# Attention kernel on one core: the last two key/value blocks are made within the first attention steps, and the second pair's queries wait in DRAM

## The chip, the cores and the metric

The kernel runs on 1 core of a Trainium2 chip. The metric is the device time of one execution in microseconds; lower is better. Matrix products run on TensorE (PE in the profile), the other engines are VectorE (DVE), ScalarE (ACT) and GpSimd (POOL). SyncE (SP) does no arithmetic here: it issues every DMA, in one queue, in order.

## The reference

It is one inference step of a streaming encoder with two layers, for a prompt of 1024 rows and a sample of 32 rows, of width 1024. Layer 0 is a matrix-memory mixer with an MLP. Layer 1 attends in chunks of 64 rows to keys and values that all layers of its kind would share; they are made from the output x of layer 0. Cut to the part that the change touches:

```python
kv = (x * (1 + kv_scale) + kv_shift) @ p['w_kv']          # 1024 -> 256 keys, 256 values
k_sh = kv[..., :KV_W].reshape(Bsz, S, NKV_B, HD_B)        # 4 heads of 64
v_sh = kv[..., KV_W:].reshape(Bsz, S, NKV_B, HD_B)
q = (u @ p['w_q_b'][lb]).reshape(Bsz, S, NH_B, HD_B)      # 16 heads of 64
...
s = jnp.einsum('bqkgd,bskd->bkgqs', qb, kb).astype(jnp.float32) * (HD_B ** -0.5) + bias
s = jnp.where(valid, s, -jnp.inf)
p = jax.nn.softmax(s, axis=-1).astype(vb.dtype)
return jnp.einsum('bkgqs,bskd->bqkgd', p, vb)
...
y = o @ p['w_out_b'][lb]
```

A chunk of queries sees its own chunk of keys and the eight before it, 576 keys at most, with a learned bias by relative position. The sample sees 512 cached keys and its own 32. The last 512 rows of keys and values, and the sample's, are outputs as well.

## The kernel before

**Tiles and parts.** Tokens lie in three blocks of 384, 384 and 288 columns (`TBS`); for keys and values in nine tiles of 128, the ninth holding the sample's 32 rows. A float32 factor is kept as a high part (a rounded copy, made by ACT) and a low part (the rest, made by DVE); `split` (L89, L90) makes both. A product is three matmuls: high by high, high by low, low by high. The three parts of a projection have lines L118 to L120.

**The stages around the change**, in order of time:

- *Queries*, L1412 to L1441. Eight strips of 128 columns, two heads each (`fc`, two to a weight block `pr`), are computed for three token blocks, first for the weight blocks 0, 1, 2 and then for 3. An eviction writes a high part (ACT, L1439) and a low part (DVE, L1440) into `QOT[ti]`, a tile for each token block. Meanwhile the norm that ends layer 0 runs for the next block on ACT (L889 to L891) and DVE (L892 to L896), stores x (L1401) and makes the block's inputs `U` (ACT L326 and L330, DVE L331).
- *Keys and values*, L1449 to L1526. Four blocks of `w_kv` are loaded and split into buffers of the tag "wc". For a tile t, `kv_input` loads x (L1482), scales it on POOL and shifts it on DVE, and splits it into `uk`, two tiles ahead. 48 products follow: for keys (i = 0) and then values (i = 1), for each of eight row blocks k, the three parts in turn (L1509, L1510, L1511). `put_keys` splits the keys (L1456, L1457), transposes them on PE (L1462) and copies them into `k0`, `k1` (L1467). `cached_keys` does the same with the cache, in every other tile. Tiles 4 to 8 store keys and values (L1523, L1524).
- *Bias*, L1541 and L1545: four tiles of the relative bias, in "wc" too.
- *Attention*, L1552 to L1664. The four key heads form two pairs (`gp`), `e` counts within a pair. `softmax_unit` makes scores (L1558), adds the bias with the maximum (DVE, L1569), the exponential (ACT, L1572), the reciprocal (L1573) and the scaling (POOL). `transposed` turns the probabilities round on PE (L1588) and copies them out (ACT L1596 for e = 1, DVE L1598 for e = 0). `weighted_values` multiplies by the values (L1608) and writes over the queries (L1613, L1614).
- *Output projection*, from 1632 us on.

**Buffers.** The pool `ring` has 3 buffers "raw" and 6 buffers "wc". Of the eight banks of PSUM, attention uses two double ones for scores, three for transposes (tag "pt") and one for values.

**What sets the order.** Side work is written as generators that `flow.tick` moves on between steps. In attention PE's order is the written one (`manual_schedule`): a group of scores is added, and older groups move on by one step, to transposes and values; chunks alternate between wide ones (8, 12, 13, ...) and slim ones (7, 6, 5, ...), all for the first pair and then all for the second. Everything else is ordered by the scheduler of the language, by priorities and free buffers.

## Time and profile before

| what | us |
|---|---|
| median of 3 runs (lowest, highest) | 2479.54 (2476.41, 2479.93) |
| profiled execution, its own time | 2479.81 |
| its span | 2478.0 |
| queries, within the span | 1263.5 to 1359.3 |
| keys and values | 1359.3 to 1422.0 |
| attention | 1422 to 1632 |

The times are of whole executions. The span runs from the first to the last recorded instruction of one profiled execution, whose granted clock of TensorE was 0.992 of full speed on average. Places in the text ("at 1423") are microseconds from the start of this span. The page of the profile gives totals, groups of instructions by line, and the chain of work that ended last; an answer of the trace gives the same for a stretch of time.

### The profile page before, as it was taken

The numbers are of one execution on the slowest core, as the hardware profiler recorded it, in microseconds if no ns is written. First come the engines' busy times: TensorE is split into PE (matmuls) and PEld (weight loads), VectorE is DVE, ScalarE is ACT, GpSimd is POOL, SyncE is SP. The second block draws the span as 40 slices with busy tenths as digits, with TensorE's granted clock in tenths as the row PEclk, the third lists the DMA queues.
The fourth block names the chain that finished last, engine by engine and source line by source line (L and its number), as shares of the span: only waits on it lengthen the run. The fifth ranks groups of instructions, "written<-read, shape, count | busy, mean of one in ns | idle before, by whom it ended". The sixth has DMA issues, their size and how long they took to land.

```text
span 2478.0 us, 42688 instructions
## 1 busy us (share of the span) xinstructions
PE 2413.7 (97%) x16844; PEld 2315.4 (93%) x16844; DVE 1759.7 (71%) x4038; ACT 1016.9 (41%) x2118; POOL 168.6 (7%) x315
## 2 busy tenths in 40 slices
PE   7999999999999999999999999999999999999997
PEld 4999999999999999999999867789999999899997
DVE  4899999788679679677597667746853442776758
ACT  4644456382211212212266556654754443221212
POOL 0211100000000000000001134410000000000003
PEclk9999999999999999999999989999999999999999
DMA  8433224313224224234122310050375646767632
GB/s 297 122 110 101 84 88 129 107 35 119 77 87 137 84 86 135 80 92 142 43 98 82 91 40 1 18 147 27 134 251 212 215 179 254 262 239 273 255 130 72
DMA packets 236220, 318.10 MB, mean 128 GB/s; under 512 B 11624, under 2 KB 185084, under 8 KB 234996
## 3 DMA queue, kind: packets, MB, share of 16 engines
q1 hardware_dynamic: 236020, 315.38, 38.8%
q8 instruction: 132, 2.16, 0.4%
q14 instruction: 68, 0.56, 0.1%
HBM read 242.79 MB, written 74.91 MB: 128 GB/s over the span
## 4 chain that ended last, share of the span: by engine, by line
PE 78%; DVE 8%; DMA 6%; ACT 2%; issue 1%; POOL 0%; SPq 0%; DVEq 0%; POOLq 0%; ACTq 0%
PE up L118 10%; PE up L120 10%; PE up L119 9%; PE dn L1283 9%; PE dn L119 5%; PE dn L118 5%; PE dn L120 5%; DMA fx<-hd 3%; PE pv L1608 2%; PE pt L1588 2%; PE s L1558 2%; PE o L118 1%; PE o L119 1%; PE o L120 1%; PE op_b L118 1%
## 5 line engine op out<-in xcount | busy, mean ns | idle before, releaser
L120 PE MATMUL up<-u,w_up 128*128 128x264 f32 x1024 | 292.9, 286 | 0.0
L118 PE MATMUL up<-u,w_up 128*128 128x264 f32 x1024 | 292.4, 286 | 0.0
L119 PE MATMUL up<-u,w_up 128*128 128x264 f32 x1024 | 291.1, 284 | 0.0
L1283 PE MATMUL dn<-fx,wf 128*128 128x264 f32 x2208 | 275.3, 286 | 7.9 <-DMA fx<-hd 7.4
L1283 PEld LDWEIGHTS dn<-fx,wf 128*128 128x128 f32 x2208 | 272.2, 189 | 9.7 <-issue 4.6
L119 PE MATMUL dn<-h,w_dn 128*128 128x384 f32 (+1 forms) x768 | 249.5, 325 | 0.0
L118 PE MATMUL up<-U,w_up 128*128 128x384 f32 (+1 forms) x768 | 249.2, 324 | 0.0
L119 PE MATMUL up<-U,w_up 128*128 128x384 f32 (+1 forms) x768 | 247.9, 323 | 0.0
L118 PE MATMUL dn<-h,w_dn 128*128 128x384 f32 (+1 forms) x768 | 247.8, 323 | 0.0
L120 PE MATMUL up<-U,w_up 128*128 128x384 f32 (+1 forms) x768 | 247.6, 322 | 0.0
L120 PE MATMUL dn<-h,w_dn 128*128 128x384 f32 (+1 forms) x768 | 247.3, 322 | 0.0
L119 PEld LDWEIGHTS up<-u,w_up 128*128 128x128 f32 x1024 | 193.9, 189 | 0.0
L118 PEld LDWEIGHTS up<-u,w_up 128*128 128x128 f32 x1024 | 193.8, 189 | 0.0
L120 PEld LDWEIGHTS up<-u,w_up 128*128 128x128 f32 x1024 | 193.3, 189 | 0.0
L986 DVE SCALAR_TENSOR_TENSOR ACC<-dn,ada,ACC 128x264 f32<-128x264 f32 (+4 forms) x328 | 131.7, 426 | 86.4 <-PE dn L1283 74.6
L238 DVE SCALAR_TENSOR_TENSOR aacc<-rada,cs,aacc 128x256 f32<-128x256 f32 x448 | 190.3, 477 | 0.0
L986 DVE SCALAR_TENSOR_TENSOR acc<-dn,ada,acc 128x384 f32<-128x384 f32 (+2 forms) x256 | 119.4, 486 | 47.4 <-PE dn L120 46.3
L1025 ACT ACTIVATE r<-up 128x384 f32<-128x384 f32 (+1 forms) x96 | 44.3, 463 | 246.9 <-PE up L120 238.4
L119 PEld LDWEIGHTS dn<-h,w_dn 128*128 128x128 f32 x768 | 144.4, 188 | 0.2 <-DVE h L1028 0.2
L120 PEld LDWEIGHTS dn<-h,w_dn 128*128 128x128 f32 x768 | 144.5, 188 | 0.0
L120 PEld LDWEIGHTS up<-U,w_up 128*128 128x128 f32 x768 | 144.3, 188 | 0.0
L118 PEld LDWEIGHTS up<-U,w_up 128*128 128x128 f32 x768 | 144.2, 188 | 0.1
(354 smaller groups left out, 5957.4 us busy)
## 6 DMA issues: line engine op xcount, KB each, us to landing
hd<-HL SPq DMA_DIRECT2D x28, 1848.0 KB
raw_up<-in_w_up_dram SPq DMA_DIRECT2D x68, 512.0 KB
rada<-in_w_ada_dram SPq DMA_DIRECT2D x64, 512.0 KB
fx<-hd SPq DMA_DIRECT2D x37, 528.0 KB
raw_dn<-in_w_down_dram SPq DMA_DIRECT2D x36, 512.0 KB
ada_room<-in_w_ada_dram SPq DMA_DIRECT2D x32, 512.0 KB
fx<-hd SPq DMA_DIRECT2D x50, 264.0 KB
fx<-hd SPq DMA_DIRECT2D x16, 792.0 KB
```

The costliest lines, as they stand in the source:

```text
L118: nc.tensor.matmul(ps, wh, mov(0, k), start=(k == 0), stop=False)
L119: nc.tensor.matmul(ps, wh, mov(1, k), start=False, stop=False)
L120: nc.tensor.matmul(ps, wl, mov(0, k), start=False, stop=(k == nk - 1))
L238: nc.vector.scalar_tensor_tensor(acc[:, cnd], raw[:, k], sc, acc[:, cnd], op0=ALU.mult, op1=ALU.add)
L986: nc.vector.scalar_tensor_tensor(xs, ps[:, off + o:off + o + mm_], gate[:, fc, cnd:cnd + 1], xs, op0=ALU.mult, op1=ALU.add)
L1025: nc.scalar.activation(r, ps[:, :n], AF.Relu)
L1283: nc.tensor.matmul(p, ws[w][:, wl, k], t[:, s0, xl], start=first and k + n_ == 0, stop=k == kg - 1 and n_ == 2, skip_group_check=not first)
L1558: nc.tensor.matmul(s[:, b, :w], qst, kk[i][:, g, k0 + j0:k0 + j0 + w], start=(i == 0), stop=(i == 1))
L1588: nc.tensor.transpose(pt[:kp, j - j0, pr * P:(pr + 1) * P], ps_[pr][:, j * P:j * P + kp], ident)
L1608: nc.tensor.matmul(pv[64 * e:64 * e + 64, :nq], V[:kp, vt0 + j, g * 64:(g + 1) * 64], pts[e][:kp, j, :nq], start=(j == 0), stop=(j == nt - 1))
```

## The change

It does five things.

1. The weight blocks of the queries come in the order 2, 3, 0 and then 1. `QOT[ti]` is laid out so that each pair's queries lie together. The second pair's queries (high and low) are stored to DRAM (`qd`, 1.57, 1.57 and 1.31 MB) as soon as its last strip is evicted.
2. The blocks of `w_kv` are loaded and split into the room that those queries left, not into "wc" buffers. So more inputs `uk` fit.
3. The stage of keys and values makes only tiles 0 to 6 (`LATE = 7`). In a tile, the 32 products with high parts of x go first, then the 16 with low parts. Cached keys come one per tile.
4. Tiles 7 and 8 are made in pieces of 6 products within the first attention steps. `fill` is called at each group of a step and puts out a piece at every second call. Their accumulator, `KVB`, takes one bank of the three that transposes had.
5. Only two bias tiles are loaded at first. When the pieces are done, `second_pair` gives the bank back as a third room ("pt3"), loads the second pair's queries back and loads the other two bias tiles. The first block of output weights is loaded one step earlier and split one step later.

```diff
+    qd = [dr.tile([P, 2, 6 if ti < 2 else 5, 256], F32, name=f"qd{ti}") for ti in range(3)]
+    def qo(c, gp):
+        return QOT[c // 6][:, gp, :, c % 6, :]
...
+    def kv_block(pr, half, dst):
+        nm = f"kv{pr}_{half}"
+        raw = raw_tile([P, 4, 256], f"raw_{nm}")
+        nc.sync.dma_start(raw, a["w_kv"][512 * half:512 * half + 512, 256 * pr:256 * pr + 256].rearrange(
+            "(k p) c -> p k c", p=P))
+        split(dst[0], dst[1], raw)
+        wkv[pr, half] = dst
+    def rooms(ti, n):
+        flat = QOT[ti][:, 1].rearrange("p e c x -> p (e c x)")
+        return [flat[:, i * 1024:(i + 1) * 1024].rearrange("p (k c) -> p k c", k=4) for i in range(n)]
+    for gi, grp in enumerate(((2, 3, 0), (1,))):
...
+                if fc == 7:
+                    nc.sync.dma_start(qd[ti], QOT[ti][:, 1].bitcast(F32))
                 flow.tick(n / 96)
+            if gi:
+                if ti == 0:
+                    r0 = rooms(0, 3)
+                    kv_block(0, 0, r0[0:2])
+                elif ti == 1:
+                    r1 = rooms(1, 3)
+                    kv_block(0, 1, r1[0:2])
+                    kv_block(1, 0, (r0[2], r1[2]))
+                else:
+                    kv_block(1, 1, rooms(2, 2))
...
-    wkv = [[wblock(f"kv{pr}_{half}", a["w_kv"], 512 * half, 256 * pr) for half in range(2)] for pr in range(2)]
...
-    uks = [kv_input(0), kv_input(1)]
+    uks = {t: kv_input(t) for t in range(2)}
+    LATE = 7
...
+    def kv_mm(pk, uk, i, k, part):
+        w = wkv[i, k // 4]
+        if part == 0:
+            nc.tensor.matmul(pk, uk[:, 0, k], w[0][:, k % 4], start=(k == 0), stop=False)
+            nc.tensor.matmul(pk, uk[:, 0, k], w[1][:, k % 4], start=False, stop=False)
+        else:
+            nc.tensor.matmul(pk, uk[:, 1, k], w[0][:, k % 4], start=False, stop=(k == KC - 1))
...
+    def late_keys(kd, t, m, pos):
+        yield
+        put_keys(kd, bank(f"kt_n{t}"), m, pos)
+    for t in range(LATE):
+        if t < 4:
+            flow.add(cached_keys(t))
+        m, pos, vi, dk, dv, r0 = kv_place(t)
...
+        for part in range(2):
+            for i in range(2):
+                for k in range(KC):
+                    kv_mm(pk[i], uk, i, k, part)
+                if i != part:
+                    flow.tick()
+        kd = [tmp_t([P, 256], f"kd{i}_n{t}", F32R) for i in range(2)]
+        split_keys(kd, pk[0], m)
+        flow.add(late_keys(kd, t, m, pos))
...
+    psX_cm = tc.tile_pool(name="psX", bufs=1, space=PSUM, reuse_waits="tile")
+    KVB = psX_cm.__enter__().tile([P, 2, 256], F32, name="KVB")
+    def kv_tile(t):
+        m, pos, vi, dk, dv, r0 = kv_place(t)
+        uk = uks.pop(t)
+        for i in range(2):
+            pk = KVB[:, i]
+            for k in range(KC):
+                kv_mm(pk, uk, i, k, 0)
+                kv_mm(pk, uk, i, k, 1)
+                if k % 2 == 0:
+                    continue
+                if k == KC - 1 and i == 0:
+                    work = raw_tile([P, 4, 256], f"kd_{t}")
+                    kd = kd_of(work)
+                    split_keys(kd, pk[:m], m)
+                    nc.scalar.copy(work[:m, 2], pk[:m])
+                    put_rows(dk, r0, m, work[:m, 2])
+                elif k == KC - 1:
+                    nc.scalar.copy(V[:m, vi], pk[:m])
+                    put_rows(dv, r0, m, V[:m, vi])
+                yield
+                if k == 3 and i == 1:
+                    put_keys(kd, psT.tile([P, 2, 256], F32, tag="pt", name=f"kt_n{t}", bufs=2).rearrange(
+                        "p i c -> p (i c)"), m, pos)
+                    yield
+        done_kv.add(t)
+    def kv_pieces():
+        for t in range(LATE, NT):
+            yield from kv_tile(t)
+    done_kv = set(range(LATE))
+    pieces = kv_pieces()
+    fills = [0, 0.0]
+    def fill(share):
+        if fills[0] is None:
+            return
+        fills[1] += share
+        while fills[0] < fills[1]:
+            if next(pieces, fill) is fill:
+                fills[0] = None
+                return
+            fills[0] += 1
...
-    for i, (nb, ns) in enumerate(((3, 0), (3, 0), (2, 1), (0, 3))):
+    def bias_tile(i):
+        nb, ns = ((3, 0), (1, 2))[i % 2]
...
+    bias_tile(0)
+    bias_tile(1)
+    nun = [0, 0]
+    psY = []
...
+            nun[1] += 1
+            if psY and nun[1] % 3 == 0:
+                pt = psY[0].tile([P, 2, 256], F32, tag="pt3", name=f"pt_{nm}_{e}_{j0}", bufs=1)
+            else:
+                pt = psT.tile([P, 2, 256], F32, tag="pt", name=f"pt_{nm}_{e}_{j0}", bufs=2)
             js = range(j0, min(nt, j0 + 2))
+            if j0 == 4:
+                fill(0.5)
...
+        if nt <= 4:
+            fill(0.5)
...
+        fill(0.5)
         pts[gp, c, e] = transposed(pr_, wid, e, nm)
         yield
         if e:
+            fill(0.5)
...
+    def second_pair():
+        psX_cm.__exit__(None, None, None)
+        psY_cm.append(tc.tile_pool(name="psY", bufs=1, space=PSUM, reuse_waits="tile"))
+        psY.append(psY_cm[0].__enter__())
+        for ti in range(3):
+            nc.sync.dma_start(QOT[ti][:, 1].bitcast(F32), qd[ti])
+        bias_tile(2)
+        bias_tile(3)
...
+                while not gp and min(c // 2, 8) not in done_kv:
+                    fill(1.0)
                 for e in range(2):
                     flow.add(att_group(gp, c, e))
                     flow.tick()
-                if gp and i in (8, 11):
-                    wo_pre[0, len(wo_pre)] = wo_block(0, len(wo_pre))
+                    if fills[0] is None and not psY:
+                        second_pair()
+                if gp and i in (7, 10):
+                    wo_raw = raw_tile([P, 4, 256], f"raw_ob0_{len(wo_pre)}")
+                    for dst, src in wo_srcs(wo_raw, 0, len(wo_pre)):
+                        nc.sync.dma_start(dst, src)
+                if gp and i in (9, 12):
+                    w = ring.tile([P, 2, 4, 256], F32R, tag="wc", name=f"w_ob0_{len(wo_pre)}", bufs=6)
+                    split(w[:, 0], w[:, 1], wo_raw)
+                    wo_pre[0, len(wo_pre)] = w
```

The number of evictions, score products, softmaxes and transposes stays the same.

On ACT, in the queries' stage, around the norm of the third token block. In the names, `w1_n01_2` is that norm's work, `QO0` the queries of the first token block, and `raw_kv0_0` the first weight block of keys and values. Before:

```order
L330 ACTIVATE ut_n01_1_7_0_13407<-acc0_1_5247,comb_92 128x384
L889 ACTIVATE w1_n01_2_13415<-var_n01_2_13412,eps_ln_75 128x288
L1439 CAST QO0_13196<-q_5_0_13440 64x6x64
L890 ACTIVATE w1_n01_2_13415<-w1_n01_2_13415 128x288
L891 ACTIVATE w1_n01_2_13415<-w1_n01_2_13415 128x288
```

And after:

```order
L330 ACTIVATE ut_n01_1_7_0_13411<-acc0_1_5247,comb_92 128x384
L889 ACTIVATE w1_n01_2_13419<-var_n01_2_13416,eps_ln_75 128x288
L1458 CAST QO0_13199<-q_1_0_13444 64x6x64
L890 ACTIVATE w1_n01_2_13419<-w1_n01_2_13419 128x288
L89 CAST QO0_13199<-raw_kv0_0_13979 128x1024
L891 ACTIVATE w1_n01_2_13419<-w1_n01_2_13419 128x288
```

The cast of the weight block now stands between two instructions of the norm, and it writes into the tile from which the second pair's queries are stored.

On PE, at the start of attention. `s_0_7_01` are scores of pair 0, chunk 7, e = 0, second half of the heads; `pt_0_8_0_0` is a transposed tile of chunk 8; `k0`, `k1` are the keys, `uk_7` the input of tile 7. Before:

```order
L1558 MATMUL s_0_8_11_14966<-k1_14101,QO1_13490 128x288
L1558 MATMUL s_0_7_00_14977<-k0_14100,QO1_13490 128x512
L1558 MATMUL s_0_7_00_14977<-k1_14101,QO1_13490 128x512
L1558 MATMUL s_0_7_01_14986<-k0_14100,QO1_13490 128x512
L1558 MATMUL s_0_7_01_14986<-k1_14101,QO1_13490 128x512
L1588 MATMUL pt_0_8_0_0_14996<-ident_64,p_0_8_00_14938 128x128
```

And after:

```order
L1666 MATMUL s_0_7_00_14832<-k0_14123,QO1_13494 128x512
L1666 MATMUL s_0_7_00_14832<-k1_14124,QO1_13494 128x512
L1666 MATMUL s_0_7_01_14841<-k0_14123,QO1_13494 128x512
L1666 MATMUL s_0_7_01_14841<-k1_14124,QO1_13494 128x512
L1541 MATMUL KVB_14775<-QO0_13199,uk_7_14667 128x256
L1542 MATMUL KVB_14775<-QO0_13199,uk_7_14667 128x256
L1544 MATMUL KVB_14775<-QO0_13199,uk_7_14667 128x256
```

The first piece (6 products in all, these three lines twice) stands between the scores and the transposes; further pieces follow in the same way, the last of the 16 pieces within the steps of chunks 14 and 5.

On SP, the bias loads and the last stores of keys (`ks`) and values (`V`). Before:

```order
L1523 DMA out_dram<-ks_14804 128x256
L1541 DMA bias_14913<-bias_d 64x3x576
L1524 DMA out_dram<-V 128x256
L1541 DMA bias_14913<-bias_d 64x3x576
L1523 DMA out_dram<-ks_14889 32x256
L1541 DMA bias_14916<-bias_d 64x3x576
L1524 DMA out_dram<-V 32x256
```

And after:

```order
L1548 DMA ck_14436<-in_cache_k_dram 128x256
L1646 DMA bias_14776<-bias_d 64x3x576 x2
L1646 DMA bias_14779<-bias_d 64x576
L1536 DMA out_dram<-V 128x256
L1646 DMA bias_14779<-bias_d 64x576
L1650 DMA bias_14779<-bias_d 32x2x544
L1536 DMA out_dram<-ks_14569 128x256
```

The first bias tile now stands ahead of every store of keys and values, and the second among the first of them.

More of the change, by code (lines that the diff above doesn't have):

```diff
@@ L1467, in put_keys, with kd_of @@
                     KCOPY[i][half != g0](dst, ps[64 * g0:64 * g0 + 64, i, :, :m])
+    def kd_of(work):
+        return [work[:, i].bitcast(F32R) for i in range(2)]
     ck, cv = a["cache_k"][0].rearrange("s g d -> s (g d)"), a["cache_v"][0].rearrange("s g d -> s (g d)")
@@ L1546, in trunk_kernel @@
                               bias_d[h0:h0 + 4 * ns - 3:4, :32, :544].rearrange("h i j -> i h j"))
-        bias += [b3[:, j] for j in range(nb)]
-        sbias += [s3[:, j] for j in range(ns)]
-    nun = [0]
+        bias.extend(b3[:, j] for j in range(nb))
+        sbias.extend(s3[:, j] for j in range(ns))
+    bias_tile(0)
+    bias_tile(1)
+    nun = [0, 0]
+    psY = []
     def softmax_unit(qst, g, k0, nk, bt, off, nm):
```

83 lines of the change are left out of this document (38 added, 45 removed).

## Prediction

> **What bounds the kernel now.** I read the page's engine totals first, then the busy time of each engine in the stages that the change touches, then PE's waits there, then the chain of work and the timeline at the points where a term is needed.
>
> ```profile
> PE 2413.7 (97%) x16844; PEld 2315.4 (93%) x16844; DVE 1759.7 (71%) x4038; ACT 1016.9 (41%) x2118; POOL 168.6 (7%) x315
> ```
>
> PE is busy for 97% of the span, so what counts is work taken off PE's path and the few places where PE stands still. By stage (us, then PE, PEld, DVE, ACT and POOL busy with their counts, granted clock, DMA share, GB/s):
>
> ```profile
> 1263.50:1359.30 95.80, 95.07 (x585) 93.61 (x584) 78.10 (x143) 62.92 (x135) 7.24 (x3) 1.00 0.31 95
> 1359.30:1422.00 62.70, 58.60 (x486) 57.56 (x484) 42.96 (x79) 34.41 (x88) 12.09 (x6) 1.00 0.35 91
> 1422.00:1440.00 18.00, 11.51 (x49) 8.77 (x49) 10.21 (x35) 8.67 (x24) 5.71 (x8) 0.70 0.66 150
> 1440.00:1530.00 90.00, 87.54 (x654) 64.90 (x653) 62.54 (x224) 57.65 (x166) 36.64 (x72) 0.98 0.00 1
> 1530.00:1632.00 102.00, 97.59 (x722) 71.68 (x721) 74.35 (x262) 69.10 (x198) 43.39 (x84) 1.00 0.08 18
> ```
>
> These are the queries' projection, the keys and values, the start of attention, and attention's two halves. PE is full in the first. In the second it loses 4.1 us. In the third it loses 6.5 of 18 us, and its clock falls to 0.70. PE's waits in the second stage and, below, at the start of attention:
>
> ```profile
> PE kv L1511 <- DVE uk L90: 4.1, 4, 2.1
> PE s L1558 <- DVE mx L1569: 4.1, 2, 3.1
> PE pt L1588 <- DVE pT L1598: 1.7, 1, 1.7
> ```
>
> The chain of waits says what the longest of them, 3.1 us, hangs on: a bias tile, whose load starts after the last store of values.
>
> ```profile
> 1423.54 6.78 DMA bias<-bias_d
> 1430.48 0.76 DVE L1569 CUSTOM_DVE_ANT_0 p<-s,bias 128x576 f32<-128x576 f32 x1 [2.45 <-DMA bias<-bias_d]
> 1431.30 1.22 PE L1558 MATMUL s<-k,QO 128*128 128x512 f32 x2 [3.15 <-DVE mx L1569]
> ```
>
> **The change part by part.** All terms are made against the profiled execution's 2479.81 us (its span is 2478.0), 0.27 us above the median of 2479.54, so the sum is not corrected. I call "same" what lies within 0.2% (4.96 us): about what a measurement of this kernel can tell from no change.
>
> *Term 1: the keys' and values' stage gets shorter.* Tiles 7 and 8 leave it: 2 × 48 products and 2 × 4 transposes of keys, 104 PE instructions. Their spacing comes from a full stretch of this stage, the first of these rows (the others serve terms 3 and 4):
>
> ```profile
> 1400.00:1420.00 20.00, 20.00 (x171) 20.00 (x170) 13.74 (x28) 12.08 (x34) 0.00 (x0) 1.00 0.27 70
> 1422.10:1444.50 22.40, 15.99 (x73) 11.33 (x73) 11.95 (x40) 10.44 (x27) 7.20 (x10) 0.70 0.53 120
> 1444.50:1480.00 35.50, 35.17 (x259) 26.72 (x258) 26.20 (x86) 22.64 (x62) 14.29 (x28) 1.00 0.00 1
> ```
>
> 20.00 / 171 = 117 ns, and 104 × 117 ns = 12.2 us. The products with high parts now go first, so a product with a low part (L1511 waits for it, 4.1 us) has 32 others ahead of it, 32 × 117 ns = 3.7 us, more than the longest single wait of 2.1: I take the 4.1 as gone. Late next is DVE: it still makes all nine inputs here, so its 42.96 us now stand against some 46 us of PE rather than 62.7, and cached keys come every tile, not every other. PE lost 4.1 us at 69% DVE; at over 90% it can lose between nothing and as much again; I take 1.5, under half, since inputs 0 to 5 no longer wait for the weights' buffers. Term: −12.2 − 4.1 + 1.5 = −14.8 (−16.3 to −12.2).
>
> *Term 2: the queries' stage.* Three stores (1.57, 1.57 and 1.31 MB) join it. At a DMA share of 0.31 they have room. But the first weight block of keys and values is now split in the room that the first store must leave:
>
> ```profile
> 1294.18 0.56 DVE L1440 TENSOR_TENSOR QO<-q,QO 64x384 fp32r<-64x384 f32 x1
> 1296.13 0.55 SPq L1401 DMA_DIRECT2D xsp<-acc  x1
> 1297.00:1302.00 5.00, 5.00 (x29) 4.82 (x28) 3.66 (x8) 4.94 (x10) 0.00 (x0) 1.00 0.87 315
> 1301.35 0.45 ACT L890 ACTIVATE w_n<-w_n 128x288 f32<-128x288 f32 x1
> 1301.83 0.45 ACT L891 ACTIVATE w_n<-w_n 128x288 f32<-128x288 f32 x1
> 1319.09 0.19 DVE L331 TENSOR_TENSOR U<-ut_n,U 128x32 fp32r<-128x32 f32 x1 [0.19 <-ACT ut_n L330]
> 1319.73 0.29 PE L118 MATMUL q<-U,w_q 128*128 128x288 f32 x1
> 1328.33 1.05 ACT L89 CAST w_kv<-raw_kv 128x1024 fp32r<-128x1024 f32 x1 [0.38 <-PE q L120]
> 1329.47 1.23 DVE L90 TENSOR_TENSOR w_kv<-raw_kv,w_kv 128x1024 fp32r<-128x1024 f32 x1
> ```
>
> The split costs ACT 1.05 us and DVE 1.23 us and stood, before, in quiet water at 1328. It now stands on ACT between L890 and L891 of the third block's norm (1301.8). Behind L891 on the same engine stand evictions of q and the inputs U, and PE needs the last U at 1319.73, 0.45 us after it is made (1319.28). The store can be issued when the fourth strip is evicted (1294.74); with the 0.9 us that the store of 1296.13 took to its first packets and 1.57 MB at 315 GB/s (5.0 us) it lands near 1300.7, before the split. Then U comes later by between 1.05 and 2.3 us, say 1.7; less 0.45 of slack that is +1.3 (0 to +6). The upper end is the next store sharing the 315 GB/s: 3.15 MB take 10.0 us, landing near 1305.7 to 1307, some 5 later.
>
> *Term 3: start of attention.* Only two bias tiles are loaded here, ahead of the last stores, so the 3.15 us wait goes. The stretch from the first score product to the end of the first chunk's values:
>
> ```profile
> 1422.14 0.80 PE L1558 MATMUL s<-k,QO 128*128 128x288 f32 x4
> 1438.02 1.45 PE L1588 MATMUL pt<-ident,p 128*128 128x128 f32 x10 [1.73 <-DVE pT L1598]
> 1441.20 3.35 PE L1608 MATMUL pv<-pT,V 128*64 128x256 f32 x20
> ```
>
> takes 1422.14 to 1444.55, 22.4 us. It has 15.99 us of PE work at a clock of 0.70; at full clock that would be 11.2, so 4.8 us hang on the clock. Fewer stops should win back half of it, 2.4. Into it come three pieces of 6 products, 18 × 117 ns = 2.1 us, half of them in what is left of the waits (1.73 here, the first softmaxes), leaving 1.05. Term: −3.15 − 2.4 + 1.05 = −4.5. Bounds: the whole clock and pieces all hidden, −8.0; clock as bad as before, with the pieces in full and at half speed, 0.
>
> The Trainium skill, "TensorE: Matmul & The Clock Gate", section "HAM oscillation — how this bites in real kernels", gives the shorthand "no PE-idle gaps >~3.4µs" for keeping full clock. The trace does not agree: the clock is at 0.70 here though the longest gap is 3.15 us. By that rule the start of attention, with no gap near it after the change, would run at full clock, and term 3 would be −8.0; this is within rival B.
>
> *Term 4: the moved work comes back.* Of the 96 products and 8 transposes 86 run after the first values: 86 × 117 ns = 10.1 us on PE. What they can hide in is the share of the chain that isn't PE:
>
> ```profile
> by line: PE pv L1608 36.4%; PE s L1558 24.9%; PE pt L1588 22.1%; DVE pT L1598 7.9%; issue 4.0%; DVE p L1569 3.2%; ACT QO L1613 0.8%; DVE QO L1614 0.6%; DVE mx L1569 0.4%; DVE mx L1573 0.2%
> ```
>
> PE holds 83.4% between 1440 and 1485; 16.6% of the 35.5 us of the row above is 5.9 us. A piece stands at a fixed place in PE's order, not at the stall, so I let 60% of this be filled: 3.5. Term: +6.6 (+4.2 to +10.1).
>
> *Term 5: two rooms for transposes.* The accumulator of the pieces takes the third room until they are done. Which steps that meets: chunks 8, 12 and 13 with six tiles each, 7, 6 and 5 with four, 30 tiles. A room is free again when its copy ends:
>
> ```profile
> L1598 DVE COPY pT<-pt 128x512 f32<-128x512 f32 x20 | 13.6, 684 | 2.4 <-PE pt L1588 2.4
> L1596 ACT COPY pT<-pt 128x512 f32<-128x512 f32 x20 | 11.5, 584 | 22.5 <-PE pt L1588 22.4
> ```
>
> With two rooms PE may run one copy ahead; a piece stands before each third tile (or behind the second), 6 × 117 = 702 ns, and covers the copy of the first. So most tiles pay nothing, and I take 2.0: 30 × 67 ns, a tenth of a copy (0 to +19, the worse end being a whole copy per tile: 15 × 684 + 15 × 584 ns). A few products of pieces also wait for the accumulator's eviction; that is inside it.
>
> Costed at nothing: the reload of the second pair's queries, 4.46 MB or 14.2 us at 315 GB/s, issued when the pieces end near 1480 and first needed at about 1530 by the second pair; the row 1440 to 1530 shows the DMA engines at 0.00. Without that cover it would cost up to 14 us. The two last bias tiles ride behind it (6.78 us above). The load of the output weights moves one step, in attention's second half at a DMA share of 0.08; its splits move one step the other way, among DVE's 74.35 of 102 us. If SP's queue sticks at the pieces' stores, only these loads wait behind it.
>
> Sum: −14.8 + 1.3 − 4.5 + 6.6 + 2.0 = −9.4, so 2479.8 − 9.4 = 2470.4 us.
>
> **The rivals.**
> B, a larger gain: the clock stays up and the pieces fill the stalls. −14.8 + 1.3 − 8.0 + 4.2 + 0.5 = −16.8: 2463.0. For it: the 3.15 us gap was the longest, and pieces stand where PE waited for copies. Against: the half clock lasted here through much shorter gaps too.
> C, the gain is eaten: the pieces lie wholly on the path and the clock is as bad as before. −14.8 + 1.3 + 0 + 10.1 + 2.0 = −1.4: 2478.4. For it: PE shows 35.17 of 35.50 us busy from 1444.5 on.
> E, the queries' store lands late and stops ACT in the norm: term 2 is 5.6 rather than 1.3, the rest as forecast: 2474.7. Against: the store of tile 0 is issued ahead of the next.
> D, slower: the third room was what kept PE going. Each of the 30 tiles waits a whole copy, 19.0 instead of 2.0: 2487.4. It decides (over 2484.8) from (4.96 + 11.4) / 30 = 0.55 us a tile on. For it: DVE's copies already hold 7.9% of the chain with three rooms, and pieces add evictions to DVE and ACT. Against: ACT stands idle 22.5 us before its 20 copies, and the pieces themselves give them time.
>
> **How the numbers follow.** Forecast (A) 0.40, own range 2466 to 2475; B 0.20; C 0.14; E 0.08; D 0.18. Faster by over 0.2% (below 2474.9) are B, 0.36 of A and half of E: 0.60. Within 0.2%: C, the rest of A and of E, and a little of D: 0.23. Slower: 0.17, nearly all of D. The range takes B in to 2460 and D to 2486; beyond lie perhaps 0.05 below and 0.12 above.
>
> **What the profile of the changed kernel would show.** Term 1: the stretch of keys and values near 48 us with no wait for a low part; with several us of waits for inputs, DVE is the new bound there. Term 2: a wait of PE for U at the third block, 1 to 2 us; over 4 is E. Term 3: no wait for a bias, and a clock above 0.8 in the first 18 us of attention. Term 4: the time from the first values to the last piece, against 83% PE in the chain before. Term 5: waits of transposes for L1710 and L1712, a sum of some 2 us; from 16 on D holds. I am wrong if the first half of attention grows by more than the 15 us which the stage before gives up.

## The result and the profile after

The changed kernel takes 2488.61 us (median of 6; 2484.68 to 2490.34) against 2479.66 us before (6 runs): the ratio is 1.0038, with a 95% interval of 1.0026 to 1.0051. It is slower by 9 us; 2470.4 was forecast, with a range of 2460 to 2486. The profiled execution took 2490.34 us, with a span of 2488.6.

Where the time went is read from PE's timeline: the first product of each stage marks its start. In the profiled executions of this document, of kernels written alike up to the queries, the queries begin between 1262 and 1266 us, so stages are compared by their lengths. "Start of attention" runs from the first score product to the first values product of the eighth chunk (chunk 4); it holds all pieces. In brackets is the stretch of term 3, from the first score product to the end of the first chunk's values. Forecast and measured are differences to before.

| stage, us | before | after | forecast | measured |
|---|---|---|---|---|
| queries | 95.7 | 96.0 | +1.3 | +0.3 |
| keys and values | 62.8 | 55.9 | -14.8 | -6.9 |
| start of attention (first chunk) | 64.2 (22.4) | 75.3 (16.5) | +4.1 (-4.5) | +11.1 (-5.9) |
| rest of attention | 145.6 | 148.9 | 0 | +3.3 |
| output projection | 100.2 | 100.4 | 0 | +0.2 |
| sum | 468.6 | 476.6 | -9.4 | +8.1 |

The busy times by stretch of the changed kernel, in the columns of the prediction's table:

```profile
1265.70:1361.70 96.00, 95.31 (x584) 93.49 (x583) 79.29 (x140) 62.84 (x130) 10.29 (x5) 1.00 0.46 152
1361.70:1417.60 55.90, 47.31 (x382) 46.70 (x380) 39.57 (x75) 30.57 (x81) 7.04 (x4) 0.94 0.35 91
1417.60:1435.00 17.40, 15.53 (x97) 12.21 (x98) 11.93 (x38) 10.26 (x25) 7.20 (x10) 0.90 0.02 7
1435.00:1478.00 43.00, 38.18 (x297) 31.39 (x295) 26.24 (x82) 24.11 (x65) 12.16 (x23) 1.00 0.21 80
```

Keys and values have 382 PE instructions instead of 486, as counted, but PE is busy for only 47.3 of 55.9 us: 8.6 us idle, twice the 4.1 of before. The start of attention is busier (15.5 of 17.4 us) at a clock of 0.90 rather than 0.70. While the pieces run, from 1435 to 1478, PE stands still for 4.8 of 43 us, where before it stood still for 0.3 of 35.5 us (the prediction's row from 1444.5 on). PE's waits in these two stages, first from 1361 to 1425, then from 1425 to 1480:

```profile
PE kt_n L1493 <- ACT kd_n L1485: 6.6, 1, 6.6
PE s L1666 <- DVE k L1498: 3.3, 2, 2.1
```

```profile
PE pt L1702 <- DVE pT L1712: 2.3, 4, 0.8
PE pt L1702 <- DVE k L1498: 1.6, 1, 1.6
PE KVB L1541 <- ACT kd L1606: 1.2, 2, 0.6
PE pt L1702 <- ACT pT L1710: 0.4, 2, 0.2
```

**The one wait of 6.6 us.** The wait for low parts (4.1 us) is gone, and a longer one has taken its place: the first key transposes wait for the high part of the keys. The timelines of DVE, ACT and PE, in this order, show on what that hangs:

```profile
1365.24 0.55 DVE L1459 TENSOR_TENSOR QO<-q,QO 64x384 fp32r<-64x384 f32 x1
1367.76 1.23 DVE L1522 TENSOR_TENSOR x<-x,kvss 128x1024 f32<-128x1024 f32 x1 [1.97 <-POOL x L1521]
1369.02 0.56 DVE L1459 TENSOR_TENSOR QO<-q,QO 64x384 fp32r<-64x384 f32 x1
1370.79 1.23 DVE L1522 TENSOR_TENSOR x<-x,kvss 128x1024 f32<-128x1024 f32 x1 [1.21 <-POOL x L1521]
1372.04 0.42 DVE L1459 TENSOR_TENSOR QO<-q,QO 64x256 fp32r<-64x256 f32 x1
...
1378.58 0.19 DVE L1459 TENSOR_TENSOR QO<-q,QO 64x32 fp32r<-64x32 f32 x1 [0.25 <-ACT QO L1458]
```

```profile
1372.49 0.18 ACT L1458 CAST QO<-q 64x32 fp32r<-64x32 f32 x1 [5.80 <-DVE QO L1459]
1378.57 0.37 ACT L1485 CAST kd_n<-kv 128x256 fp32r<-128x256 f32 x1
```

```profile
1379.00 1.15 PE L1493 MATMUL kt_n<-ident,kd_n 128*128 128x128 f32 x4 [6.57 <-ACT kd_n L1485]
```

The last query product ended at 1361.9, but its evictions on DVE end at 1378.8: they stand, in DVE's order, behind the shifts (L1522) of inputs 5 and 6, and these wait for POOL. ACT's evictions wait for DVE's, and the cast of the first keys stands behind them. Before, DVE had shifted three inputs by 1349 and had no fourth to shift until 1367; now the free buffers let the scheduler put inputs 2 to 6 in between. The clock falls as well; in the 4 us behind the wait it is 0.61, with 24 products, and 1.00 with 37 in the next 4:

```profile
1380.00:1384.00 4.00, 4.00 (x24) 4.00 (x24) 2.63 (x2) 3.38 (x8) 1.92 (x2) 0.61 0.00 0
1384.00:1388.00 4.00, 4.00 (x37) 4.00 (x36) 3.93 (x9) 1.32 (x5) 0.00 (x0) 1.00 0.07 19
```

**Two smaller ones.** The last tile made ahead of attention now has 128 rows of keys instead of the sample's 32, and their casts last until 1419.6: 3.3 us of waiting for `k`, against 0.5 (and 0.4 in the run without late tiles below, whose last tile is the sample's). And in the last fifth of attention PE waits for DVE's maximum; after, and before:

```profile
PE s L1666 <- DVE mx L1677: 3.6, 6, 1.5
```

```profile
PE s L1558 <- DVE mx L1569: 1.2, 5, 0.4
```

### The profile page after: what moved, and what is told of

Read it like the earlier page. It is cut to its first block, busy times and chain, and to the rows that moved or that the text cites. A ratio compares the mean times of both kernels' runs of the same rounds, so it can differ in the third digit from the quotient of the medians.

```text
span 2488.6 us, 42710 instructions
## 1 busy us (share of the span) xinstructions
PE 2415.7 (97%) x16844; PEld 2319.4 (93%) x16844; DVE 1760.6 (71%) x4039; ACT 1016.4 (41%) x2118; POOL 165.8 (7%) x315
## 5 line engine op out<-in xcount | busy, mean ns | idle before, releaser
L120 PEld LDWEIGHTS up<-U,w_up 128*128 128x128 f32 x768 | 144.3, 188 | 0.0
L118 PEld LDWEIGHTS up<-U,w_up 128*128 128x128 f32 x768 | 144.2, 188 | 0.1
L119 PEld LDWEIGHTS up<-U,w_up 128*128 128x128 f32 x768 | 144.3, 188 | 0.0
```

Source lines behind the costliest of these rows:

```text
L118: nc.tensor.matmul(ps, wh, mov(0, k), start=(k == 0), stop=False)
L119: nc.tensor.matmul(ps, wh, mov(1, k), start=False, stop=False)
L120: nc.tensor.matmul(ps, wl, mov(0, k), start=False, stop=(k == nk - 1))
```

## The experiments

All stand in one table; stage lengths are from one profiled execution each, in the first table's stages (us). The ratio is to the kernel before, from runs on the same chip.

| kernel | ratio (95%) | queries | keys, values | start of att. | rest of att. | projection | sum |
|---|---|---|---|---|---|---|---|
| before | 1 | 95.7 | 62.8 | 64.2 | 145.6 | 100.2 | 468.6 |
| after | 1.0038 (1.0026, 1.0051) | 96.0 | 55.9 | 75.3 | 148.9 | 100.4 | 476.6 |
| bias first | 1.0036 (1.0024, 1.0049) | 95.9 | 53.9 | 75.8 | 149.1 | 102.0 | 476.6 |
| no late tiles | 1.0022 (1.0012, 1.0032) | 96.0 | 67.7 | 61.2 | 149.1 | 102.0 | 475.9 |
| thin pieces | 1.0012 (1.0003, 1.0021) | 95.9 | 56.7 | 68.1 | 148.1 | 100.5 | 469.3 |
| output weights as before | 1.0031 (1.0020, 1.0042) | 96.0 | 56.4 | 75.4 | 145.6 | 100.4 | 473.7 |
| inputs behind evictions | 1.0045 (1.0031, 1.0058) | 95.8 | 55.3 | 78.0 | 149.4 | 102.0 | 480.4 |
| before, two rooms | 1.0061 (1.0048, 1.0073) | 95.8 | 63.3 | 63.8 | 159.0 | 100.4 | 482.3 |
| three mends, late tiles | 1.0027 (1.0017, 1.0036) | 95.9 | 56.6 | 75.9 | 145.7 | 100.4 | 474.5 |
| mends, no late tiles | 1.0005 (0.9996, 1.0013) | 95.9 | 66.1 | 59.8 | 145.7 | 100.4 | 467.9 |
| + paced inputs | 1.0023 (1.0013, 1.0034) | 96.0 | 68.5 | 59.8 | 145.7 | 100.5 | 470.5 |
| after + paced inputs | 1.0067 (1.0054, 1.0079) | 96.0 | 57.7 | 80.3 | 149.1 | 102.0 | 485.0 |
| paced, products in turn | 1.0031 (1.0020, 1.0043) | 96.1 | 70.7 | 60.9 | 145.9 | 100.5 | 474.1 |
| mends, shift on POOL | 1.0022 (1.0012, 1.0031) | 95.8 | 70.1 | 61.3 | 145.7 | 100.4 | 473.3 |
| **before, shift on POOL** | **0.9976 (0.9966, 0.9986)** | 96.0 | 58.5 | 61.0 | 145.6 | 100.4 | 461.5 |
| short lead, shift on POOL | 0.9983 (0.9974, 0.9992) | 98.1 | 60.2 | 57.7 | 145.5 | 100.4 | 462.0 |

The ratios follow the sums only roughly, since the rest of the program varies by some 3 us from one execution to the next.

### Bias tiles ahead of the inputs

```diff
+    bias_tile(0)
+    bias_tile(1)
     uks = {t: kv_input(t) for t in range(2)}
...
-    bias_tile(0)
-    bias_tile(1)
```

> The changed kernel with the two first bias tiles allocated and loaded ahead of the inputs of keys and values, so that two of the six buffers are taken and inputs 4, 5 and 6 can no longer be made while the last queries are evicted. Theory (queue): the wait of 6.6 us of the first key transposes for the high part of the keys comes from inputs 5 and 6 standing ahead of the last query evictions in VectorE's queue; it falls to 2 us or less, and the time from 2488.6 to 2482 to 2485. Rival (rate): the inputs can't come faster than load, GpSimd and VectorE allow, and PE then waits for inputs instead: the stage stays at 55 to 57 us and the time at 2487 to 2490.

The wait shrank and changed its releaser. PE's waits of that kernel:

```profile
PE kt_n L1493 <- DVE kd_n L1486: 3.3, 1, 3.3
PE s L1666 <- DVE k L1498: 3.0, 2, 2.1
PE kt_c L1493 <- DVE kd_c L1486: 1.3, 1, 1.3
```

6.6 us became 3.3 + 1.3, the stage 2.0 us shorter: in the direction of the queue, short of its number, and the time did not follow (2487.47 us; start of attention and projection took 2.1 us more). Shifts and splits of inputs still stood ahead of the key splits in DVE's rows.

### No late tiles

```diff
-    LATE = 7
+    LATE = 9
...
-        split_keys(kd, pk[0], m)
+        split_keys(kd, pk[0][:m], m)
...
-        uks[t + 2] = kv_input(t + 2)
+        if t + 2 < NT:
+            uks[t + 2] = kv_input(t + 2)
```

> The changed kernel with no late tiles: all nine tiles are made before attention, no pieces, third transpose room from the start; the queries still go to DRAM, products with high parts still go first. Theory (pieces lie wholly on PE's path and add waits): attention loses the 16.1 us that it grew by between the first values and the sixth slim chunk and 2.1 us at its start, the stage before gains 104 x 117 ns = 12.2 us and loses some 1.8 us of waiting for the last keys: 2488.6 - 18.2 + 12.2 - 1.8 = 2480.8 (2478 to 2483). Rival (the forecast's terms 4 and 5, a third hidden): attention loses only 10.7, the time is 2488.6 - 10.7 + 12.2 = 2490 (2488 to 2492).

The start of attention fell from 75.3 to 61.2, by 14.1 us, and the stage before grew by 11.8: late tiles cost more in attention than they save ahead of it. The time was 2484.35, between the two expectations, with 1.5 us lost in the output projection, whose cause is open.

### Thin pieces

```diff
-                kv_mm(pk, uk, i, k, 0)
-                kv_mm(pk, uk, i, k, 1)
+                if k == 0:
+                    nc.tensor.matmul(pk, uk[:, 0, k], wkv[i, 0][0][:, 0], start=True, stop=False)
+                if k == KC - 1:
+                    kv_mm(pk, uk, i, k, 1)
```

> The changed kernel with 88 of the 96 products of the pieces left out (each of the four accumulations keeps its first and its last product, so keys and values of tiles 7 and 8 are not the reference's); evictions, transposes, stores and the two rooms stay. Theory (nothing of them is hidden): 88 x 117 ns = 10.3 us go, 2478.3 (2476.5 to 2480). Rival (a third is hidden in waits, as forecast): 6.7 us go, 2481.9. Second rival (pieces cover the copies, and without them the two rooms stall): under 5 us go, over 2483.6.

The start of attention fell from 75.3 to 68.1: leaving out 88 products (10.3 us) gained 7.2. The number is near the expected third hidden, but the missing 3.1 us had not filled stalls. PE is idle for 9.3 us there with whole pieces and for 9.5 with thin ones; what fell is its busy time, by 7.5 (first row: the changed kernel, second: thin pieces):

```profile
1417.63:1492.95 75.32, 66.06 (x480) 52.82 (x480) 47.01 (x148) 41.95 (x111) 24.19 (x44) 0.98 0.28 89
1417.25:1485.33 68.08, 58.54 (x392) 43.11 (x393) 46.08 (x148) 40.48 (x111) 24.31 (x44) 0.95 0.31 99
```

Part of the 2.8 us between 10.3 and 7.5 can be the clock, 0.95 against 0.98; how much was not measured. And most of the stalls come with the late tiles: the kernel without them takes 61.2 us, 3.8 of it idle. Of the 6.9 us between it and the thin kernel, 5.8 are idle time. PE's waits in the thin kernel from 1430 to 1485 name them: a transpose room that is not yet copied out, or that the late keys hold, ACT's copies, and the accumulator:

```profile
PE pt L1704 <- DVE pT L1714: 2.3, 4, 0.8
PE pv L1726 <- ACT pT L1712: 2.0, 1, 2.0
PE pt L1704 <- DVE k L1498: 1.6, 1, 1.6
PE pt L1704 <- ACT pT L1712: 1.2, 2, 1.0
PE KVB L1599 <- ACT kd L1608: 0.8, 2, 0.5
```

The second line is not due to them alone: without late tiles PE waits as long for such a copy, only earlier, in the first chunk's values:

```profile
PE pv L1725 <- ACT pT L1711: 2.1, 1, 2.1
```

### Output weights at the steps of before

```diff
-                if gp and i in (7, 10):
-                    wo_raw = raw_tile([P, 4, 256], f"raw_ob0_{len(wo_pre)}")
-                    for dst, src in wo_srcs(wo_raw, 0, len(wo_pre)):
-                        nc.sync.dma_start(dst, src)
-                if gp and i in (9, 12):
...
+                if gp and i in (8, 11):
+                    wo_pre[0, len(wo_pre)] = wo_block(0, len(wo_pre))
```

> The changed kernel with the first block of output weights loaded and split at the steps of before. Theory (the splits' new place in VectorE's queue holds up the maximum of the scores): the three lags of 1.4, 1.2 and 1.0 us in the last fifth of attention go, the time falls by 3.3 us to 2485.3. Rival (they come from something else of the second pair, the reload or the buffers): the lags stay, 2488 to 2489.

As the theory had it: the rest of attention is back at 145.6 and the wait for the maximum in its last fifth at 1.2 us. The split of a weight block in DVE's order costs PE up to 1.5 us at one step and at most 0.4 at the step beside it. The time, 2486.28 us, is in the same direction, but its interval overlaps the changed kernel's.

### Inputs behind the query evictions

```diff
+    kvs2 = cp.tile([P, 2, KC, 2], F32, name="kvs2")
+    nc.vector.scalar_tensor_tensor(out=kvs2.rearrange("p a k c -> p (a k c)"), in0=qo(16, 0)[:, 1, 96:128].bitcast(F32),
+                                   scalar=0.0, in1=kvss.rearrange("p a k c -> p (a k c)"), op0=ALU.mult, op1=ALU.add)
+    kvsc, kvsh = kvs2[:, 0], kvs2[:, 1]
```

> The changed kernel; the scale and shift with which inputs 2 to 8 are made are first copied through an instruction that reads the last evicted queries (its value times zero is added), so that these inputs can't be made before the queries are evicted. Theory (queue): the 6.6 us wait of the first key transposes falls to 1 us or less and the stage of keys and values from 55.9 to 49 to 51 us. Rival (rate): PE waits for inputs 2 to 4 instead and the stage stays above 53 us.

Neither came true: the stage stayed at 55.3 us, but not because PE waited for inputs. The evictions were in time, and the wait went on to the next in the queue, now three waits, the longest 3.9 us:

```profile
PE kt_n L1493 <- DVE kd_n L1486: 4.9, 3, 3.9
```

So the evictions were only the first to be held up. The key split that ended the longest wait stands in DVE's order behind casts of `k`, and these behind the shift of an input, for which DVE stood still 2.5 us:

```profile
1380.52 1.22 DVE L1522 TENSOR_TENSOR x<-x,kvs 128x1024 f32<-128x1024 f32 x1 [2.47 <-POOL x L1521]
1381.66 1.72 DVE L1498 CAST k<-kt_n 64x256 fp32r<-64x256 f32 x4
1383.42 0.42 DVE L1486 TENSOR_TENSOR kd_n<-kv,kd_n 128x256 fp32r<-128x256 f32 x1
```

The hold also delays the scaling on POOL of all inputs from 2 on, so it tests the evictions, not the shifts. The start of attention grew by 2.7 us; why is open.

### The kernel before with two rooms

```diff
-            pt = psT.tile([P, 2, 256], F32, tag="pt", name=f"pt_{nm}_{e}_{j0}", bufs=3)
+            pt = psT.tile([P, 2, 256], F32, tag="pt", name=f"pt_{nm}_{e}_{j0}", bufs=2)
```

> The kernel before with two rooms for transposes, not three, and nothing else. The first seven steps of attention, 30 transposed tiles, show the price of the third room without pieces. Theory (from the run with thin pieces, where 4.9 us of stalls stood beside evictions of the accumulator): 2 to 6 us over these steps, 70 to 200 ns a tile. Rival D as forecast: over 0.55 us a tile, 16 us or more. As forecast in term 5: 2 us.

In the first seven steps the transposes waited 1.9 us for DVE's and 1.4 us for ACT's copies, 3.3 us or 0.11 us a tile (before, 1.7 us), of which the start of attention shows nothing (63.8 against 64.2). In the changed kernel, with pieces, the same two waits come to 2.7 us (above). Rival D's mechanism, 0.55 us a tile and more, is out. Later the third room counts: over the whole of attention it is worth 13 us (209.8 to 222.8).

### Mends together, with and without late tiles

With late tiles, three edits: the hold behind the evictions, the output weights as before, and the last tile's products in turn:

```diff
+        if t == LATE - 1:
+            for i in range(2):
+                for k in range(KC):
+                    for part in range(2):
+                        kv_mm(pk[i], uk, i, k, part)
+                flow.tick()
-        for part in range(2):
+        for part in range(2 if t < LATE - 1 else 0):
```

> The changed kernel with three mends: inputs behind the evictions (as in the run on that), the last tile before attention with its three products in turn as before so that its keys are done 16 products (1.9 us) sooner, and the output weights loaded and split at the steps of before. Theory (the three losses are local and add up): from the first query product to the layer's last projection 476.6 - 6.0 - 1.9 - 3.4 = 465.3 us, against 468.6 before; time 2474 to 2478. Rival (they hide one another): 469 us or more, no faster than before.

Without late tiles, the first two edits:

> As the run with three mends, but with no late tiles (all nine before attention, products with high parts first throughout). Theory (late tiles gain nothing, since pieces lie on the path): from the first query product to the layer's last projection 475.9 - 6.8 - 3.4 = 465.7 us, about what the three mends give with late tiles. Rival (late tiles are the gain and the losses were accidents of order): 3 us or more behind the run with late tiles.

The mends did not add up: 474.5, not 465.3. Only the output weights gave theirs. The last tile's products in turn made the wait for `k` longer (4.9 us): its keys were split sooner, but the casts of the last two tiles' keys then came in one row, up to 1416.1, so the casts decide there. Without late tiles the kernel takes 467.9, 6.6 us less, and 2479.32 us, level with before. This pair prices the late tiles: the stage ahead gains 9.5 us, start of attention loses 16.1. (The pair differs in the last tile's order too, which lengthened the wait for `k` by 1.6 us.)

### Pacing the inputs

Each input is held until the keys two tiles earlier are split, in the kernel without late tiles and in the changed kernel; and then with the products in turn.

```diff
+            nc.vector.scalar_tensor_tensor(out=ss.rearrange("p a k c -> p (a k c)"), in0=after, scalar=0.0,
+                                           in1=kvss.rearrange("p a k c -> p (a k c)"), op0=ALU.mult, op1=ALU.add)
...
+            uks[t + 2] = kv_input(t + 2, kd[1][:, :32].bitcast(F32))
```

> As the run with mends and no late tiles, but instead of one hold behind the last queries each input t from 2 on is held until the keys of tile t - 2 are split (its scale and shift are copied through an instruction that reads the split keys). Theory (what the first key transposes wait for is a query eviction or a key split standing behind an input's shift, which waits for GpSimd and the load): with no shift ahead of a key split the waits of key transposes fall from 5.6 us in all to under 1.5, the stage of keys and values from 66.1 to 61 to 63 us, and from the first query product to the layer's last projection it takes 463 to 465 us, against 468.6 before. Rival (the inputs need their lead): PE waits 3 us or more for the inputs' low or high parts, the stage stays at 65 us or more.

> The changed kernel (late tiles, output weights as changed) with only the pacing of the inputs. Theory: the 6.6 us wait goes, the stage falls from 55.9 to 49.5 to 51.5 us; attention keeps its 224 us, since its loss has other causes; time some 4 to 6 us under that of the changed kernel, 2483 to 2485. Rival: the stage stays above 54 us.

> As the paced run without late tiles, but with the three products of a block in turn, as before, rather than high parts first. Theory (high parts first covers the low parts' lateness, the 4.1 us that the kernel before waited): PE waits for low parts again, 1 to 4 us more in this stage than in the paced run with high parts first. Rival (with more buffers the inputs are in time anyway): no wait for them, and keys that are done 16 products sooner; the stage equal or up to 1 us shorter.

```profile
PE kv L1547 <- ACT uk L89: 5.7, 5, 3.0
PE kt_n L1493 <- DVE kd_n L1486: 1.2, 1, 1.2
```

These are the waits of the paced kernel without late tiles. The key transposes' wait fell to 1.2 us, as the theory said; but now PE waits 5.7 us for inputs, and the stage is longer: the rival's case. In the changed kernel the same happened (5.8 us for inputs, and still 3.9 for the key split), and the start of attention grew by 5 us as well. With the products in turn PE waited 3.3 us for high and 2.9 us for low parts, only 0.5 us more for inputs in all. The stage took 2.2 us more, though PE stood still less in it, 7.1 us against 7.9; what grew is its busy time, by 2.9, at a clock of 0.93 rather than 0.98 (first row: high parts first, second: in turn):

```profile
1361.62:1430.09 68.47, 60.60 (x487) 58.90 (x485) 44.13 (x85) 34.32 (x87) 12.05 (x7) 0.98 0.30 80
1361.08:1431.73 70.65, 63.54 (x486) 61.30 (x484) 44.23 (x83) 33.36 (x83) 12.12 (x7) 0.93 0.28 74
```

So high parts first was 2.2 us better here, but not by sparing PE idle time.

### The shift on POOL

One word in `kv_input`, once in the mended kernel without late tiles, once in the kernel before:

```diff
-        nc.vector.tensor_add(x, x, kvsh[:, :, cnd:cnd + 1].broadcast_to([P, KC, m]))
+        nc.gpsimd.tensor_add(x, x, kvsh[:, :, cnd:cnd + 1].broadcast_to([P, KC, m]))
```

> As the run with mends and no late tiles (inputs held behind the last queries), but the shift of an input is made on GpSimd, behind its scaling, not on VectorE. Theory (key splits stand on VectorE behind shifts that wait for GpSimd): without shifts in its queue VectorE reaches the key splits in time, the waits of key transposes fall from 5.6 us to under 2 and the stage of keys and values from 66.1 to 62 to 64 us, time 2474 to 2478. Rival (the chain of an input, load to split, is what is short, whichever engine does it): GpSimd then takes 3.8 us an input, and PE waits 4 us or more for inputs or key splits; the stage stays at 65 us or more.

> The kernel before with the shift of the inputs on GpSimd and nothing else. If the mend is one of its own and not of the change, it helps here too: the 4.1 us that PE waits for low parts fall by 1 us or more, the stage from 62.8 to 59 to 62 us. Rival: with two inputs ahead at most the chain gets longer by GpSimd's 1.9 - 1.2 = 0.7 us an input, and the stage stays at 62.5 to 65.

In the kernel before it gives the lowest time of the study: 2472.09 us, ratio 0.9976. Its stage of keys and values, and PE's one wait there:

```profile
1359.63:1418.11 58.48, 57.98 (x486) 57.38 (x484) 41.85 (x74) 34.67 (x88) 22.93 (x12) 1.00 0.38 97
```

```profile
PE kv L1511 <- DVE uk L90: 0.4, 1, 0.4
```

PE is busy for 57.98 of 58.48 us. In the kernel before DVE had stood still for 12.0 us of this stage ahead of five shifts, for POOL, as its groups of instructions show; those rows are gone:

```profile
L1488 DVE TENSOR_TENSOR x<-x,kvss 128x1024 f32<-128x1024 f32 x5 | 6.1, 1225 | 12.0 <-POOL x L1487 12.0
```

The start of attention got 3.2 us shorter as well: the longest wait for the maximum there fell from 3.1 to 1.6 us, and the clock in its first 18 us was 0.81 instead of 0.70.

In the mended kernel, where inputs run free behind the evictions, it made the stage longer, 70.1 instead of 66.1 us, as the rival had it: 5.4 us of waits of cached keys' transposes for DVE's key split, which stands behind the splits of inputs 2, 3 and 4.

### A short lead as well

Three bias tiles allocated ahead of the inputs, no late tiles, output weights as before, and the shift on POOL:

```diff
+    for i in range(3):
+        bias_tile(i)
     uks = {t: kv_input(t) for t in range(2)}
```

> Of the change stay the queries in DRAM, the early bias, high parts first; no late tiles, output weights as before, the shift on GpSimd; three bias tiles are allocated ahead of the inputs, so that an input runs at most three tiles ahead. Theory (inputs made far ahead stand in the way of key splits; with short lead and without shifts on VectorE neither side waits): waits in the stage of keys and values under 2 us, the stage 58 to 60 us as in the kernel before with the shift moved, and the start of attention 1 to 4 us shorter than there by the early bias: from the first query product to the layer's last projection 458 to 461 us against 461.5, time 2468 to 2473. Rival (the run-ahead is not the cause): the stage stays at 65 us or more, as in the run with the shift moved and all inputs free.

2474.56 us, ratio 0.9983: faster than before. The stage is 60.2 us, against 70.1 with free inputs; the waits ahead of it and at its end:

```profile
PE kv L1559 <- ACT uk L89: 2.1, 1, 2.1
PE s L1667 <- ACT ks L1596: 0.9, 1, 0.9
```

The run with 70.1 us differs from this one in two things, the lead and the hold behind the evictions, for which POOL stood still there:

```profile
1362.42 3.77 POOL L1521 TENSOR_TENSOR x<-x,kvs 128x1024 f32<-128x1024 f32 x2 [16.31 <-DVE kvs L1528]
```

So a short lead without a hold gives a short stage; which of the two decides no run shows. That the lead counts for something, the run with bias tiles first shows (53.9 against 55.9). The start of attention, 57.7 us, is the shortest of all, 3.3 us under the one-word kernel, which the queries' stage gives back (98.1, with 2.1 of it the wait for the first input). That the one-word kernel is the better of the two is not shown: their intervals overlap.

## Why the prediction was wrong, by its own steps

From -9.4 to +8.1 are about 17.5 us: 7.9 in term 1, 7.0 in terms 3 to 5, 3.3 in what was costed at nothing, less 1.0 in term 2, and 0.2 in the projection.

**Term 1** (-14.8, measured -6.9) failed at two steps. "I take the 4.1 as gone": the wait for low parts did go, but what caused it stayed. It was never the products' order alone: DVE idled for POOL ahead of the shifts, 12 us within the stage of before. I had set its 42.96 busy us against PE's time and not asked what DVE itself waits for; with the shift on POOL alone, the kernel before waits 0.4 us. And "1.5, under half, since inputs 0 to 5 no longer wait for the weights' buffers" had the sign wrong: that those inputs no longer wait is what put them ahead of evictions and key splits in an in-order queue. The order of DVE's rows stood in the built kernel and would have told it. The 104 instructions did leave. The last keys' casts, 3.3 us of wait, were not in the sum at all. The 1.5 became 8.6 us of idle time: 6.6, and 2.05 of these 3.3 that lie within the stage. The 0.8 us left is busy time, at a clock of 0.94.

**Term 2** (+1.3, measured +0.3): the split stood between L890 and L891 as said, and U came some 2 us later within the stage. PE did not wait longer, since the scheduler had moved six products of the next strip ahead of the first strip's last three, and three more ahead of its last two. The cover was PE's own order, which the term left out.

**Term 3** (-4.5, measured -5.9) was right in mechanism, with the bias wait gone and the clock at 0.90 instead of 0.70. The mended kernel without late tiles shows it without pieces, where the term would be -5.55: its start of attention is 4.4 us shorter than before, with a new wait of 2.1 us for a copy by ACT in it. The upper bound was added up wrongly: -3.15 and three pieces at half speed (4.2) are +1.05, not 0.

**Terms 4 and 5** (+8.6; with the 1.05 us of pieces in term 3, 9.7): measured 16.1 by the pair with and without late tiles. What failed is the step "What they can hide in is the share of the chain that isn't PE", 5.9 us taken from a kernel without pieces. That share is no idle time of PE: the row behind it, 1444.5 to 1480, has 35.17 of 35.50 us busy, so there were 0.3 us to fill. And the pieces did not shorten PE's idle time but added to it. The start of attention in that pair, with late tiles and without:

```profile
1414.46:1490.32 75.86, 66.97 (x480) 53.79 (x481) 46.90 (x148) 41.63 (x110) 24.28 (x44) 0.96 0.28 87
1426.97:1486.72 59.75, 55.28 (x377) 40.08 (x377) 42.27 (x141) 36.47 (x100) 24.30 (x44) 0.97 0.32 98
```

PE's busy time rises by 11.7 us and its idle time by 4.4, from 4.5 to 8.9: net, nothing is hidden, and stalls come on top. Term 5's 2.0 for the rooms as such agrees with the run on two rooms (1.6 us more of waits than before). The accumulator (1.2) was taken as "inside it" and was not; late keys in a transpose room (1.6) no term has. ACT's copies of chunk 14, which come behind two exponentials (2.0), no term has either, but without late tiles there is such a wait elsewhere (2.1). How the 4.4 us divide among these is not shown.

**Costed at nothing**: the splits of output weights, 3.3 us. "Among DVE's 74.35 of 102 us" is a share of busy time; it says nothing of which row a split stands ahead of. The reload of the queries and the last bias tiles did cost nothing.

**The rivals.** D named 2487.4, within 1.2 us of the median, by a mechanism that the run on two rooms refutes. The number is a coincidence. C's pieces wholly on the path were the nearest to the truth, but with a loss in the stage ahead that no rival had. That 0.17 stood for "slower" was too little for a change that reorders four engines.

## What to carry to other kernels

Work that fills stalls must not bring its own: price moved work with all its buffers, evictions and copies, and against stalls of the kernel that has it. More buffers are not free where engines work in order: inputs made far ahead stand in front of what is due, so look at the order of the rows, not at shares of busy time. And ask what a waiting engine waits for: one word, which moved an instruction to the engine it waited for, won 0.24% over the kernel before, and the change none.

## What the runs showed of the hardware

DVE and POOL stretch one another. The shift of an input takes DVE 1.23 us alone and 2.91 us when POOL scales the next one; POOL's 1.91 us twice became 4.45:

```profile
1354.45 1.23 DVE L1522 TENSOR_TENSOR x<-x,kvss 128x1024 f32<-128x1024 f32 x1 [2.02 <-POOL x L1521]
1357.48 2.91 DVE L1522 TENSOR_TENSOR x<-x,kvss 128x1024 f32<-128x1024 f32 x1 [1.21 <-POOL x L1521]
```

```profile
1354.86 4.45 POOL L1521 TENSOR_TENSOR x<-x,kvss 128x1024 f32<-128x1024 f32 x2 [0.44 <-DMA x<-xsp]
```

POOL's pair ends at 1359.31, and DVE's shift 1.08 us later, about its time alone. The Trainium skill, "SBUF — State Buffer", section "SBUF: two separate sides", says that a DVE instruction with two inputs in SBUF and a GpSimd one that reads SBUF share a pair of ports as an exclusive lock: the one that starts first has it for its whole instruction, and the other is blocked. These rows agree.

The clock fell without a long gap. In the changed kernel it was at 0.59 after waits of 2.05 and 1.29 us at the first scores; in the kernel with a short lead, where no wait at the start of attention is over 1.4 us, it stayed at 1.00:

```profile
1420.00:1424.00 4.00, 4.00 (x15) 2.97 (x14) 3.16 (x11) 3.12 (x7) 1.13 (x2) 0.59 0.02 4
```

```profile
1423.60:1441.60 18.00, 14.56 (x93) 10.65 (x94) 13.38 (x44) 10.26 (x29) 7.46 (x12) 1.00 0.75 276
```

The rule that the prediction weighed (the Trainium skill, "TensorE: Matmul & The Clock Gate", section "HAM oscillation — how this bites in real kernels") would have kept the first of these at full clock; the trace does not agree. Nor does the length of one wait decide. Behind a wait of 2.07 us, ending at 1363.45 in the kernel with a short lead, the clock was at 0.51 for 3.4 us (first row); behind one of 2.08 us, ending at 1381.98 in the kernel before, it stayed at 1.00 (second row):

```profile
1363.40:1366.80 3.40, 3.35 (x16) 3.35 (x17) 3.31 (x3) 1.82 (x4) 3.06 (x2) 0.51 0.44 114
1382.00:1386.00 4.00, 4.00 (x34) 4.00 (x35) 3.88 (x10) 0.00 (x0) 0.00 (x0) 1.00 0.52 131
```

How much idle time within which stretch it takes was not measured.
